# Expert weights of 128 tokens: scattered through DRAM by indirect DMAs in place of one-hot matmuls

## The chip, the cores and the metric

One core of a Trainium2 chip. The metric is device microseconds of one execution; three executions of the kernel before were timed.

## The reference

A decoder layer over 256 tokens of width 1024: modulated RMSNorm, two token mixers (pooling and attention) merged by gates, output projection, and then the part that the change touches, a product-key expert layer with 128 x 128 = 16,384 experts:

```python
q = (hf @ w_q).reshape(T, 8, 2, 128)
s = jnp.einsum('thpd,hpnd->thpn', q, sub_keys)
sv, si = lax.top_k(s, 16)
cand = sv[:, :, 0, :, None] + sv[:, :, 1, None, :]
cand_idx = si[:, :, 0, :, None] * 128 + si[:, :, 1, None, :]
cv, ci = lax.top_k(cand.reshape(T, 8, 256), 16)
expert = jnp.take_along_axis(cand_idx.reshape(T, 8, 256), ci, axis=-1)
g = jax.nn.softmax(cv, axis=-1)
a = gelu(einsum('cd,chkd->chk', x_c, u_tab[expert]))
out = einsum('chk,chkd->cd', g * a, v_tab[expert])
```

Each token picks 8 x 16 = 128 experts, each with a softmax weight.

## The kernel before, in words

The kernel gathers nothing. It computes the activation of all 16,384 experts for all tokens, multiplies by a weight that is zero where an expert was not picked, and multiplies by the whole table v. The stages, one after another on TensorE (PE): the input projections; 16 gate tiles (L517 to L527), with attention, pooling and the modulation dots run beside them in slices; 8 branch tiles; 8 output tiles; 16 query tiles with scores; 128 **u tiles** (the loop at L877); 128 **v tiles** (the loop at L941); the end.

Every weight tile is 128 x 1024 fp32. SP's queue loads it into `raw`, ACT rounds it into `whi` (L95), DVE takes the rest into `wlo` (L96), and PE multiplies with both. `Feed` (L107) keeps two tiles ahead; `raw`, `whi` and `wlo` have three buffers each in the u and v stages.

A u tile i makes 24 matmuls of 256 columns (`product`, L341) into one PSUM bank and a Gelu into `act[:, i, :]`, of shape 128 experts x 256 tokens. The weights must come into that layout, expert j on the partition, i and token along it. For that the selection (`selection`, `best`) runs on DVE in slices between the other steps: `Side` holds a generator whose yields are costs, and every tile adds a credit (SIDE_Q, SIDE_U) that buys slices. Before, it treats 4 heads for both halves of the tokens (tt = 1 and 0) as soon as their scores are there, then the other 4 heads. When it is done, `turn_picks` (L742) transposes both halves of the picks by 3 matmuls each, and then, one group of 4 tokens (GRP) per u tile, for 64 u tiles:

- `rows_of`: DVE compares a row of numbers with the picks and writes one-hot matrices `oh` (L760);
- `weigh_rows`: ACT scales one of them by the softmax weights, 4 instructions (L774);
- `spread`: PE multiplies the one-hots, 4 products of 128 x 128 by 128 in fp32, 8 matmuls in the trace (L780); the result is the 128 x 128 weight matrix of each token, in PSUM;
- `meet` (L790): DVE multiplies the act rows that are done; `wait_for_act` (L794): ACT puts the weights into the rows that are not done yet, and `late_mult` (L874) multiplies those by their Gelu when it comes.

A v tile i makes 16 matmuls (L938, L939) into eight accumulators. `weigh_act` splits two rows of act into a `w` tile (tag "w", three buffers, shared with `oh`) two v tiles ahead.

The order of instructions is the program's own on SP and POOL, on DVE from the branch stage on, and on PE and ACT in the u and v stages. POOL's queue carries 24 fetches of modulation weights (`mod_sections`, L362; `mraw`, three buffers), and between them copies `tick` of one column (`after`, L385) that wait for a gate, branch or score tile so that the queue keeps step with PE. The fetched `mraw` are consumed on DVE (L171).

Of the kernel before, what the change touches and what calls it, by code (L numbers as in the profile page):

```python
# [9 lines left out]
F32 = mybir.dt.float32  # L10
# [9 lines left out]
P = 128  # L20
# [13 lines left out]
LAG = 3  # L34
GRP = 4


# [14 lines left out]
MOD_G = 1.5  # L52
MOD_O = 1
SIDE_Q = 1.6
SIDE_U = 1.45
# [3 lines left out]
def layer_kernel(ctx: ExitStack, tc: tile.TileContext, A):  # L59
# [327 lines left out]
    after(h1[:, KD - 1, 1, 0:1].bitcast(F32))  # L387

    mask = const_load("mask", "mask", [P, P], mix)
    ident16 = mix.tile([P, P], BF16, name="ident16")  # L390
# [126 lines left out]
    for m in range(16):  # L517
        hi, lo = split(load(A["w_gate"][m]))
        ps = bank(f"gate{m}")
        product(ps[:, :T], hi, lo, h1, range(KD), step=lambda: side.add(SIDE_A / 2))  # L520
        S.activation(gate[:, m, :], ps[:, :T], AF.Tanh, scale=0.5)
        side.add(SIDE_A / 2)
        if m > 1:
            after(gate[:, m - 2, 0:1])
        if m == FIRST - 2:
            mods_side.add(0.5)
        if m >= FIRST:  # L527
            mods_side.add(MOD_G)
# [12 lines left out]
    for m in range(KD):  # L541
# [15 lines left out]
        if m > 0:  # L557
            after(merged[:, m - 1, 1, 0:1].bitcast(F32))

    warm = post.tile([P, 1], F32, name="warm")  # L560
# [117 lines left out]

    def selection(h):
        for tt in (1, 0):  # L680
            yield from pairs(tt, slice(h, h + GH))
        for h0 in range(h, h + GH, HG):
            for tt in (1, 0):
                yield from best(tt, h0)

    def best(tt, h0):
# [40 lines left out]
        V.tensor_copy(e[:, 0], ef[:, hs].rearrange("p h k -> p (h k)"))  # L727
        V.tensor_scalar(e[:, 1], e[:, 0], 7, None, op0=ALU.logical_shift_right)
        V.tensor_scalar(e[:, 2], e[:, 0], NK - 1, None, op0=ALU.bitwise_and)
        V.tensor_copy(g_e[tt][:, :, sl], e[:, 1:3])  # L730
        yield 0.6


    g_e = [scratch(2, P) for tt in range(2)]
    g_w = [scratch(P) for tt in range(2)]
    picks = big.tile([P, 3, T], F32, name="picks")
    row = big.tile([P, NK], F32, name="row")
# [3 lines left out]
    def turn_picks():  # L741
        for tt in range(2):  # L742
            ps = bank(f"picks{tt}")
            for c, src in enumerate((g_e[tt][:, 0, :], g_e[tt][:, 1, :], g_w[tt])):
                PE.transpose(ps[:, c * P : (c + 1) * P], src, ident)
            S.activation(
                picks[:, :, tt * P : (tt + 1) * P], ps[:, : 3 * P].rearrange("p (c t) -> p c t", c=3), AF.Copy
            )

    spreads = {}
    groups = T // GRP

# [60 lines left out]
    def chosen(j):  # L815
        side.extend(halves(j))
        if j % (2 * GH) == 2 * GH - 1:
            side.extend(selection((j + 1) // 2 - GH))

# [3 lines left out]
    def queries(m):  # L823
        qTs.append(work.tile([P, T], F32, tag="t", name=f"qT{m}", bufs=2))
        S.activation(qTs[m], ps_q[m][:, :T], AF.Copy)
        if m > 0:
            score(m - 1, qTs[m - 1])
            after(scores[:, m - 1, 0, 0:1])
        if m > SLAG:
            j = m - SLAG - 1  # L830
            chosen(j)
        side.add(SIDE_Q)

# [23 lines left out]

    ws = {}


# [18 lines left out]
    for i in range(NK):  # L879
# [27 lines left out]
        if some or LAG <= ready <= LAG + 1:  # L907
            rows_of(met + 1 if some else ready - LAG)
        if i == NK - 1:
            weigh_act(0)  # L910
# [30 lines left out]
    for i in range(NK):  # L941
# [4 lines left out]
        else:  # L946
            last.append((i, hi, lo, ws[i]))
        feed.ahead()
        if i % 2 == 0 and i + 2 < NK:
            weigh_act(i + 2)  # L950
        if i == 3:
            S.activation(warm2, eps, AF.Sqrt)
# [127 lines left out]
```

## Time and profile before

| | us |
|---|---|
| median of 3 executions | 1055.78 (1052.14 to 1056.24) |
| the profiled execution, its own time | 1057.16 |
| its span, first to last instruction | 1055.1 |
| PE busy | 1028.0 |
| DVE busy | 766.3 |
| ACT busy | 586.3 |
| POOL busy | 39.9 |

The span is what the profile shows; the execution's own time has 2.06 us around it. Busy PE means that matmuls are in flight; since PE is busy nearly all the time, a stage is read by what each of its tiles costs on PE and by whether another engine comes near its pace.

### The profile page before, as it was taken

To read this page: it belongs to the slowest core of one execution; us is meant where nothing else is said; L and a number is where in the kernel's file an instruction comes from. 1 tells how busy PE (TensorE), PEld (TensorE's weight loads), DVE (VectorE), ACT (ScalarE), POOL (GpSimd) and SP (SyncE) were. 2 spreads that over 40 slices of the span, in tenths; PEclk is the share of its full clock that TensorE was granted. 3 is DMA by queue.
4 is the path that set the end of the run, shared out by engine and by line. 5 is a ranking of instruction groups with operands and counts; after the bars stand their busy time and mean duration, and the time that the engine had idled before them with its cause. 6 is when DMAs were issued, how large, how long until landed. Compare 5 with 4: busy or idle time off the path is not lost.

```text
span 1055.1 us, 18956 instructions
## 1 busy us (share of the span) xinstructions
PE 1028.0 (97%) x7352; PEld 958.6 (91%) x7352; DVE 766.3 (73%) x1440; ACT 586.3 (56%) x1104; POOL 39.9 (4%) x69
## 2 busy tenths in 40 slices
PE   6999989899999999999999999999999999999997
PEld 4878989899999999999999999988888888888886
DVE  7966768797999998777788888555556555555555
ACT  4465444545664566777777777454444444444444
POOL 0012312011000000000000000000000000000000
PEclk8999989999999999999999999999999999999999
DMA  9977856365566656444444444566666665566651
GB/s 331 340 244 250 296 180 215 130 195 155 175 188 184 185 175 187 154 140 141 142 141 142 143 142 144 187 219 219 203 203 211 206 203 192 183 184 191 184 183 57
DMA packets 55965, 199.01 MB, mean 189 GB/s; under 512 B 7106, under 2 KB 7234, under 8 KB 55876
## 3 DMA queue, kind: packets, MB, share of 16 engines
q1 hardware_dynamic: 52420, 185.23, 55.0%
q0 software_dynamic: 3456, 12.58, 3.3%
q8 instruction: 57, 0.93, 0.4%
q14 instruction: 32, 0.26, 0.1%
HBM read 196.73 MB, written 1.05 MB: 187 GB/s over the span
## 4 chain that ended last, share of the span: by engine, by line
PE 90%; DVE 5%; ACT 2%; issue 1%; DMA 1%; SPq 0%; DVEq 0%; ACTq 0%; POOLq 0%; POOL 0%
PE acc L938 23%; PE acc L939 11%; PE u L347 10%; PE u L345 10%; PE u L346 10%; PE spread L780 5%; DVE wlo L96 2%; PE in L302 1%; PE in L303 1%; PE in L304 1%; PE gate L345 1%; PE gate L346 1%; PE gate L347 1%; PE q L345 1%; PE q L347 1%
## 5 line engine op out<-in xcount | busy, mean ns | idle before, releaser
L96 DVE TENSOR_TENSOR wlo<-raw,whi 128x1024 fp32r<-128x1024 f32 x320 | 390.8, 1223 | 238.1 <-ACT whi L95 237.9
L95 ACT ACTIVATE whi<-raw 128x1024 fp32r<-128x1024 f32 x320 | 338.2, 1059 | 256.7 <-PE acc L938 187.2
L938 PE MATMUL acc<-w,whi 128*128 128x512 f32 x1024 | 362.7, 399 | 0.8 <-DVE w L96 0.8
L345 PE MATMUL u<-h,whi 128*128 128x256 f32 x1024 | 293.4, 286 | 0.0
L347 PE MATMUL u<-h,wlo 128*128 128x256 f32 x1024 | 288.0, 281 | 1.0 <-DVE wlo L96 1.0
L939 PE MATMUL acc<-w,wlo 128*128 128x256 f32 x1024 | 287.8, 281 | 0.0
L346 PE MATMUL u<-h,whi 128*128 128x256 f32 x1024 | 287.8, 281 | 0.0
L938 PEld LDWEIGHTS acc<-w,whi 128*128 128x128 f32 x1024 | 192.4, 188 | 48.8 <-DVE w L96 1.0
L347 PEld LDWEIGHTS u<-h,wlo 128*128 128x128 f32 x1024 | 193.0, 189 | 1.4 <-DVE wlo L96 1.4
L939 PEld LDWEIGHTS acc<-w,wlo 128*128 128x128 f32 x1024 | 193.4, 189 | 0.0
L345 PEld LDWEIGHTS u<-h,whi 128*128 128x128 f32 x1024 | 193.1, 189 | 0.0
L346 PEld LDWEIGHTS u<-h,whi 128*128 128x128 f32 x1024 | 193.1, 189 | 0.0
L774 ACT ACTIVATE oh<-oh,picks 128x128 f32<-128x128 f32 x256 | 82.0, 407 | 0.0
L760 DVE TENSOR_TENSOR oh<-row,picks 128x1024 f32<-128x1024 f32 x64 | 78.0, 1219 | 0.0
L917 ACT ACTIVATE act<-u 128x256 f32<-128x256 f32 (+32 forms) x121 | 39.4, 325 | 58.2 <-PE u L347 58.0
L780 PE MATMUL spread<-oh 128*128 128x128 f32 x512 | 67.4, 275 | 0.0
L780 PEld LDWEIGHTS spread<-oh 128*128 128x128 f32 x512 | 62.6, 191 | 0.0
L914 ACT ACTIVATE gl<-u 128x256 f32<-128x256 f32 (+32 forms) x70 | 20.1, 288 | 73.6 <-PE u L347 66.9
L171 DVE SCALAR_TENSOR_TENSOR mraw<-mraw,c_act 128x1024 f32<-128x1024 f32 x32 | 39.0, 1219 | 12.8 <-DMA mraw<-in_w_mod 12.8
L96 DVE TENSOR_TENSOR w<-act,w 128x512 fp32r<-128x512 f32 x64 | 43.8, 685 | 0.0
L345 PE MATMUL gate<-h,whi 128*128 128x256 f32 x128 | 39.4, 308 | 0.2 <-ACT whi L95 0.2
L95 ACT ACTIVATE w<-act 128x512 fp32r<-128x512 f32 x64 | 39.4, 616 | 0.0
(254 smaller groups left out, 1191.9 us busy)
## 6 DMA issues: line engine op xcount, KB each, us to landing
raw<-in_u SPq DMA_DIRECT2D x128, 512.0 KB, 3.5
raw<-in_v SPq DMA_DIRECT2D x128, 512.0 KB, 3.6
mraw<-in_w_mod POOLq DMA_DIRECT2D x24, 512.0 KB, 4.9
raw<-in_w_gate SPq DMA_DIRECT2D x16, 512.0 KB, 4.7
raw<-in_w_q SPq DMA_DIRECT2D x16, 512.0 KB, 4.0
raw<-in_w_mod SPq DMA_DIRECT2D x8, 512.0 KB, 5.5
mraw<-in_w_mod SPq DMA_DIRECT2D x8, 512.0 KB, 6.6
raw<-in_w_qk SPq DMA_DIRECT2D x8, 512.0 KB, 6.7
```

The costliest lines, as they stand in the source:

```text
L95: S.activation(hi, t, AF.Copy)
L96: V.tensor_tensor(lo, t, hi.bitcast(F32), op=ALU.subtract)
L171: V.scalar_tensor_tensor(w, w, 1.0, c_act, op0=ALU.mult, op1=ALU.mult, accum_out=out)
L345: PE.matmul(o, hi[:, sl], hT[:, k, 0, 0:n], start=(j == 0), stop=False)
L346: PE.matmul(o, hi[:, sl], hT[:, k, 1, 0:n], start=False, stop=False)
L347: PE.matmul(o, lo[:, sl], hT[:, k, 0, 0:n], start=False, stop=(j == last))
L760: V.tensor_tensor(oh, row[:, None, None, :].to_broadcast([P, 2, GRP, NK]), picks[:, :2, sl, None].to_broadcast([P, 2, GRP, NK]), op=ALU.is ...
L774: S.activation(oh[:, 0, j, :], oh[:, 0, j, :], AF.Copy, scale=picks[:, 2, t : t + 1])
L780: PE.matmul(ps[:, j * NK : (j + 1) * NK], oh[:, 1, j, :], oh[:, 0, j, :], start=True, stop=True)
L917: S.activation(act[:, i, n:], ps[:, n:T], AF.Gelu)
L938: PE.matmul(acc[m], hi[:, sl], w, start=(i == 0), stop=False)
L939: PE.matmul(acc[m][:, T:], lo[:, sl], w[:, 0, :], start=False, stop=(i == NK - 1))
```

## The change

The second half of the tokens (tt = 1, tokens 128 to 255) gets its weights another way. A DRAM tensor `wt` of 128 x 128 x 128 floats (8 MB) is zeroed early by 16 DMAs on POOL's queue, each a 512 KB write from a 128 x 128 tile of zeros read eight times over (`clear`), bought by credits at the gate, branch and query tiles. The selection is reordered: all 8 heads of tt = 1 first, then those of tt = 0. As soon as a pair of heads of tt = 1 is selected, `place` issues 16 indirect DMAs per head on POOL, each of 128 single floats, one per partition, to addresses in `g_at`, adding to what is there (two heads may pick the same expert). That is 128 indirect DMAs. Only tt = 0 is spread by matmuls: 32 groups in place of 64. In the v stage, SP's queue fetches `wt` back in 16 pieces of 8 rows (`fetch`, 512 KB, into a "w" buffer), and DVE multiplies 8 half rows of act by each (`weigh_half`).

```diff
+IW = 8
+CLR_G = 0.25
+CLR_B = 0.3
+CLR_Q = 1
...
+    def clear():
+        for q in range(16):
+            G.dma_start(A["wt"][:, 8 * q : 8 * q + 8, :], zero[:, None, :].to_broadcast([P, 8, P]))
+            yield 1
+    clear_side = Side(clear())
...
-    def selection(h):
-        for tt in (1, 0):
-            yield from pairs(tt, slice(h, h + GH))
+    def selection(tt, h):
+        yield from pairs(tt, slice(h, h + GH))
         for h0 in range(h, h + GH, HG):
-            for tt in (1, 0):
-                yield from best(tt, h0)
+            yield from best(tt, h0)
+            if tt == 1:
+                for h1 in range(h0, h0 + HG):
+                    place(h1)
...
+        else:
+            V.tensor_scalar(e[:, 1], e[:, 0], NK - 1, 14, op0=ALU.bitwise_and, op1=ALU.logical_shift_left)
+            V.tensor_scalar(e[:, 2], e[:, 0], 7, 7, op0=ALU.logical_shift_right, op1=ALU.logical_shift_left)
+            V.tensor_tensor(e[:, 1], e[:, 1], e[:, 2], op=ALU.bitwise_or)
+            V.tensor_tensor(g_at[:, sl], e[:, 1], token.to_broadcast([P, n]), op=ALU.bitwise_or)
...
+    def place(h):
+        rows = A["wt"].rearrange("j i (t o) -> (j i t) o", o=1)
+        mine = []
+        for s in range(h * TOPK, (h + 1) * TOPK):
+            d = G.indirect_dma_start(
+                out=rows, out_offset=bass.IndirectOffsetOnAxis(ap=g_at[:, s : s + 1], axis=0),
+                in_=g_w[1][:, s : s + 1], in_offset=None, compute_op=ALU.add,
+            )
+            for e in mine:
+                tc.declare_no_dep(d.ins, e.ins, reason="experts of one head differ, and so do tokens")
+            mine.append(d)
...
-    groups = T // GRP
+    groups = P // GRP
...
         if j % (2 * GH) == 2 * GH - 1:
-            side.extend(selection((j + 1) // 2 - GH))
+            side.extend(selection(1, (j + 1) // 2 - GH))
+        if j == 2 * H - 1:
+            side.extend(*(selection(0, h) for h in range(0, H, GH)))
...
+    def fetch(i):
+        wts[i] = work.tile([P, IW, P], F32, tag="w", name=uid("wt"), bufs=3)
+        nc.sync.dma_start(wts[i], A["wt"][:, i : i + IW, :])
+    def weigh_half(i):
+        a = act[:, i : i + IW, P:]
+        V.tensor_tensor(a, a, wts.pop(i), op=ALU.mult)
...
+        if i == NK - 4:
+            fetch(0)
+        if i == NK - 2:
+            weigh_half(0)
...
         feed.ahead()
+        if i % IW == IW // 2 and i + IW // 2 < NK:
+            weigh_half(i + IW // 2)
         if i % 2 == 0 and i + 2 < NK:
             weigh_act(i + 2)
+        if i % IW == 0 and i + IW < NK:
+            fetch(i + IW)
```

What moves, in three places. First POOL's queue late in the gate stage, where the fetches `mraw` stand between copies; before:

```order
L385 COPY tick<-gate 128x1
L362 DMA mraw_1339<-in_w_mod 128x1024
L385 COPY tick<-gate 128x1
L362 DMA mraw_1392<-in_w_mod 128x1024
L362 DMA mraw_1395<-in_w_mod 128x1024
```

and now:

```order
L389 COPY tick<-gate 128x1
L396 DMA wt<-zero 128x8x128
L366 DMA mraw_1343<-in_w_mod 128x1024
L389 COPY tick<-gate 128x1
L366 DMA mraw_1396<-in_w_mod 128x1024
```

One of the 16 zeroing DMAs now stands ahead of a fetch. Four are issued in the gate stage, a fifth at its end, two in the branch stage, nine with the queries. The second place is DVE in the middle of the u stage (`wlo` is the split of a u tile, `act` here is scratch of the selection), at the end of the fourth and last pair of heads of tt = 1:

```order
L739 TENSOR_REDUCE act<-g_w_2201 128x2
L740 RECIPROCAL act<-act 128x2
L741 TENSOR_TENSOR g_w_2201<-g_w_2201,act 128x32
L743 CAST act<-act 128x32
L749 TENSOR_SCALAR act<-act 128x32
L750 TENSOR_SCALAR act<-act 128x32
L751 TENSOR_TENSOR act<-act 128x32
L752 TENSOR_TENSOR g_at<-act,token 128x32
L686 CAST act<-act 128x128
L687 TENSOR_SCALAR act<-act 128x4x16
L100 TENSOR_TENSOR wlo_4276<-raw_4273,whi_4275 128x1024
```

The four writes of `g_at` release 32 indirect DMAs each; between them and the first `oh` there are 54, 49, 31 and 26 splits of tiles. The selection of tt = 0 begins only behind the fourth. The third place is SP's queue in the v stage; before it has a load per tile, now every eighth tile a fetch between two of them:

```order
L89 DMA raw_9100<-in_v 128x1024
L89 DMA raw_9123<-in_v 128x1024
L906 DMA wt_9132<-wt 128x1024
L89 DMA raw_9150<-in_v 128x1024
L89 DMA raw_9172<-in_v 128x1024
```

The fetch for rows i + 8 stands behind the load of v tile i + 2 and ahead of that of i + 3, and takes the buffer of the `w` tile of rows i - 2 and i - 1. On PE the order is the old one less three transposes of picks and the last 32 groups of spread matmuls; the first spread stands at the same u tile.

## Rows read from the trace of the kernel before

**Rows 1.** The page: span, and each engine's busy time.

```profile
span 1055.1 us, 18956 instructions
...
PE 1028.0 (97%) x7352; PEld 958.6 (91%) x7352; DVE 766.3 (73%) x1440; ACT 586.3 (56%) x1104; POOL 39.9 (4%) x69
```

**Rows 2.** Chain that ended last: shares by line.

```profile
PE acc L938 23%; PE acc L939 11%; PE u L347 10%; PE u L345 10%; PE u L346 10%; PE spread L780 5%; DVE wlo L96 2%; PE in L302 1%; PE in L303 1%; PE in L304 1%; PE gate L345 1%; PE gate L346 1%; PE gate L347 1%; PE q L345 1%; PE q L347 1%
```

**Rows 3.** Table by stage: busy us (instructions), granted clock, DMA share, GB/s.

```profile
core 0: us, PE busy (x) PEld busy (x) DVE busy (x) ACT busy (x) POOL busy (x), PEclk, DMA share, GB/s
...
258.70:350.00 91.30, 91.30 (x774) 91.30 (x773) 87.14 (x278) 51.41 (x75) 0.00 (x0) 1.00 0.59 181
350.00:416.00 66.00, 64.96 (x547) 64.55 (x546) 61.40 (x168) 41.71 (x58) 0.00 (x0) 1.00 0.59 180
422.00:658.80 236.80, 236.80 (x2030) 236.80 (x2030) 189.21 (x252) 173.51 (x507) 0.00 (x0) 1.00 0.46 143
680.00:864.00 184.00, 184.00 (x1042) 159.46 (x1043) 108.97 (x117) 87.17 (x101) 0.00 (x0) 1.00 0.67 212
864.00:1040.00 176.00, 176.00 (x1002) 152.72 (x1000) 95.76 (x98) 81.61 (x95) 0.00 (x0) 1.00 0.57 177
```

**Rows 4.** Chain in order of time, picks, first and last spread: start us, us, what.

```profile
416.47 0.66 PE picks L745 x6
422.82 0.89 PE spread L780 x8
...
658.23 0.89 PE spread L780 x8
```

**Rows 5.** Timeline of PE, first matmuls of two tiles without spread: start us, us.

```profile
664.64 0.28 PE L345 MATMUL u<-h,whi 128*128 128x256 f32 x1
...
667.48 0.28 PE L345 MATMUL u<-h,whi 128*128 128x256 f32 x1
```

**Rows 6.** The line that fetches on POOL's queue: ns min/median/max, landing us.

```profile
L362 POOL DMA_DIRECT2D mraw<-in_w_mod x24: 527/527/681, 76.5 to 183.7; - x24
...
DMA to landing us min/median/max: 3.8/4.9/7.5
```

**Rows 7.** Chain in the gate stage, in order of time: start us, us, what.

```profile
125.62 6.73 DMA mraw<-in_w_mod
...
133.61 0.40 DVE mixed L497
...
136.65 1.22 PE mix L495 x2
137.87 0.21 PE gate L345
```

**Rows 8.** POOL's small copies between gate tiles: ns min/median/max.

```profile
L385 POOL COPY tick<-gate x14: 183/456/1266, 73.3 to 137.9; 128x1 f32<-128x1 f32 x14
```

**Rows 9.** DVE's groups from 260 to 412 us: busy us, mean ns | idle.

```profile
L96 DVE TENSOR_TENSOR wlo<-raw,whi 128x1024 fp32r<-128x1024 f32 x52 | 63.3, 1217 | 8.0 <-ACT whi L95 8.0
...
L728 DVE TENSOR_SCALAR act<-act 128x32 int32<-128x32 int32 x7 | 1.3, 182 | 0.2
```

**Rows 10.** Loads of one line on SP's queue, 864 to 1030 us.

```profile
L85 SPq DMA_DIRECT2D raw<-in_v x58: 327/328/328, 866.1 to 1027.2; - x58
...
DMA to landing us min/median/max: 3.3/3.6/4.5
```

**Rows 11.** Timelines of ACT, then of DVE, in the v stage.

```profile
900.49 1.06 ACT L95 ACTIVATE whi<-raw 128x1024 fp32r<-128x1024 f32 x1 [1.76 <-PE acc L938]
...
903.32 1.06 ACT L95 ACTIVATE whi<-raw 128x1024 fp32r<-128x1024 f32 x1 [1.25 <-PE acc L938]
...
901.58 1.23 DVE L96 TENSOR_TENSOR wlo<-raw,whi 128x1024 fp32r<-128x1024 f32 x1 [1.60 <-ACT whi L95]
```

**Rows 12.** The page's main DMA queue, and its slowest class of large loads.

```profile
q1 hardware_dynamic: 52420, 185.23, 55.0%
...
raw<-in_w_qk SPq DMA_DIRECT2D x8, 512.0 KB, 6.7
```

More of the change, by code (lines that the diff above doesn't have):

```diff
@@ L524, in layer_kernel @@
             after(gate[:, m - 2, 0:1])
+        clear_side.add(CLR_G)
         if m == FIRST - 2:
@@ L558, in layer_kernel @@
             after(merged[:, m - 1, 1, 0:1].bitcast(F32))
+        clear_side.add(CLR_B)
     warm = post.tile([P, 1], F32, name="warm")
@@ L727, in best @@
         V.tensor_copy(e[:, 0], ef[:, hs].rearrange("p h k -> p (h k)"))
-        V.tensor_scalar(e[:, 1], e[:, 0], 7, None, op0=ALU.logical_shift_right)
-        V.tensor_scalar(e[:, 2], e[:, 0], NK - 1, None, op0=ALU.bitwise_and)
-        V.tensor_copy(g_e[tt][:, :, sl], e[:, 1:3])
+        if tt == 0:
+            V.tensor_scalar(e[:, 1], e[:, 0], 7, None, op0=ALU.logical_shift_right)
+            V.tensor_scalar(e[:, 2], e[:, 0], NK - 1, None, op0=ALU.bitwise_and)
+            V.tensor_copy(g_e[:, :, sl], e[:, 1:3])
+        else:
[3 more added lines that the diff above has]
+            V.tensor_tensor(g_at[:, sl], e[:, 1], token.to_broadcast([P, n]), op=ALU.bitwise_or)
         yield 0.6
-    g_e = [scratch(2, P) for tt in range(2)]
-    g_w = [scratch(P) for tt in range(2)]
-    picks = big.tile([P, 3, T], F32, name="picks")
+    g_e = scratch(2, P)
+    g_w = [scratch(P), keep.tile([P, P], F32, name="g_w1")]
+    picks = big.tile([P, 3, P], F32, name="picks")
     row = big.tile([P, NK], F32, name="row")
@@ L741, in turn_picks @@
     def turn_picks():
[L742 to L747, printed above, removed]
-            )
+        ps = bank("picks")
+        for c, src in enumerate((g_e[:, 0, :], g_e[:, 1, :], g_w[0])):
+            PE.transpose(ps[:, c * P : (c + 1) * P], src, ident)
+        S.activation(picks, ps[:, : 3 * P].rearrange("p (c t) -> p c t", c=3), AF.Copy)
+    g_at = keep.tile([P, P], I32, name="g_at")
+    token = keep.tile([P, 1], I32, name="token")
+    G.iota(token, pattern=[[0, 1]], base=0, channel_multiplier=1)
+    def place(h):
[5 more added lines that the diff above has]
+                in_=g_w[1][:, s : s + 1], in_offset=None, compute_op=ALU.add,
+            )
+            for e in mine:
+                tc.declare_no_dep(d.ins, e.ins, reason="experts of one head differ, and so do tokens")
+            mine.append(d)
     spreads = {}
-    groups = T // GRP
+    groups = P // GRP
     def rows_of(g):
@@ L827, in queries @@
             score(m - 1, qTs[m - 1])
-            after(scores[:, m - 1, 0, 0:1])
+            if not clear_side.done:
+                after(scores[:, m - 1, 0, 0:1])
+        clear_side.add(CLR_Q)
         if m > SLAG:
@@ L858, in layer_kernel @@
     ws = {}
+    wts = {}
+    def fetch(i):
[4 more added lines that the diff above has]
+        V.tensor_tensor(a, a, wts.pop(i), op=ALU.mult)
     def weigh_act(i):
@@ L1073 @@
         aps[name] = nc.dram_tensor(f"in_{name}", a.shape, mybir.dt.from_np(a.dtype), kind="ExternalInput").ap()
+    aps["wt"] = nc.dram_tensor("wt", (NK, NK, P), F32, kind="Internal").ap()
     aps["c_act"] = nc.dram_tensor("c_act", (1, D), F32, kind="Internal").ap()
```

## The prediction

> **What bounds the kernel now.** The page comes first: TensorE (PE) is busy 1028.0 of 1055.1 us, DVE 766.3, ACT 586.3, POOL 39.9 [rows 1]. The chain of work that ended last says the same by line: v matmuls 34%, u matmuls 30%, and, the term of this change, the spread matmuls 5% [rows 2]. Then the table by stage, since a share of the whole hides a stage in which another engine is tight [rows 3]. From 422 to 659 us, where the spreads run, PE is never idle, DVE is busy 189.2 of 236.8 us and ACT 173.5: nobody else binds, so a matmul taken out there is time. From 259 to 416 us, the stage of the selection, PE is also full, but DVE is busy 87.1 of 91.3 us and then 61.4 of 66.0: 8.8 us of air in 157. From 680 us on DVE has 41 to 46% free and the DMA engines are at a share of 0.67, later 0.57.
>
> **What the change removes.** In the chain, first and last spread start at 422.82 and 658.23 us [rows 4]; there are 64, so a u tile with its spread takes 235.41 / 63 = 3.737 us. The first matmuls of two tiles without one stand 2.84 us apart [rows 5]. One spread thus costs 0.897 us; the chain's own piece says 0.89. Thirty-two of them go: 28.6 us. Three of the six transposes of the picks go too, half of 0.66 us [rows 4]: 0.3 us. Together **28.9 us**, all on PE, in a stage where PE alone sets the pace. The comparisons, scalings and multiplications that DVE and ACT lose with them are worth nothing by themselves, since PE covered them. In the v stage PE does the same as before.
>
> **What it adds, part by part.**
>
> *Zeroing.* Sixteen writes of 512 KB on POOL's queue. The nearest row is the fetch of 512 KB in 128 pieces, which held POOL for 0.53 us and landed after 3.8 to 7.5 us [rows 6]; a zeroing write is cut into 1024 pieces, so POOL needs between 0.53 and, were it by the piece, 4.2 us. It matters where POOL's queue is waited for: late in the gate stage the chain goes through a fetch issued at 125.62 that ends in a `mixed` step of DVE and a PE that starts again at 136.65, with its next matmuls at 0.21 us a piece [rows 7]. Two zeroing writes stand a little ahead of that. Each can delay it by its time on POOL and by its own transfer. A packet of the main queue costs 0.55 x 16 x 1055.1 / 52420 = 177 ns on average [rows 12], so 512 KB, 128 packets over 16 engines, take 1.4 us. Bounds: 0 (POOL is busy 4% of the time, so its queue may have the spare) and 2 x (3.7 + 1.4) = 10 us. I take **2.8 us**, the two transfers, since 0.53 us is the measured issue. The nine at the query tiles hold only POOL's copies, for which no engine waits.
>
> *Selection in another order.* The same slices with the same credits, so the spread begins at the same u tile. Each pair of heads of tt = 1 has one more small DVE step, 0.18 us [rows 9]: 4 x 0.18 = **0.7 us**, counted in full because DVE has no air there.
>
> *128 indirect DMAs.* On POOL, which has nothing else to do from 259 us on; nobody waits for them but the first fetch of `wt`. By the splits counted in the order, the four groups of 32 are released about 54, 49, 31 and 26 tiles before the picks at 416 us [rows 4], at 2.84 us a tile near 263, 277, 328 and 342 us. SP's queue reaches its first fetch at u tile 124, near 638 us with 28.9 saved. The last 64 have 310 us, 4.8 us each; POOL's time for a fetch of 128 pieces is 0.53 us [rows 6], and eight may be in flight. So **0 us** on the path. What they take from DVE is the open question. A copy of one column on POOL takes anything from 0.18 to 1.27 us [rows 8] while DVE's splits keep a mean of 1.217 us [rows 9]: it is POOL that waits for DVE. Lower end 0; upper end, DVE held for every issue: 128 x 0.53 = 68 us, less the air of 8.8, so 59 us. I take 0, by the row of the splits. The Trainium skill ("SBUF — State Buffer", SBUF: two separate sides) speaks against this: VectorE and GpSimd share a pair of SBUF ports under an exclusive lock, held for the whole instruction by whichever starts first, when a VectorE instruction with two SBUF inputs meets a GpSimd one that reads SBUF. The copies agree with the half of it in which GpSimd waits; that VectorE waits is shown by no row here.
>
> *The v stage.* Sixteen multiplications on DVE of 1024 elements with two inputs, like a split: 1.22 us each, 19.5 us in all, beside 155 us of idle DVE [rows 3]. Sixteen more fetches in SP's queue raise its traffic by an eighth. The point is their wait: fetch i + 8 takes the buffer of the `w` tile that PE uses up to tile i - 1, and the load of tile i + 3 is queued behind it. That load used to go out over two tiles earlier. Tiles are 2.83 us apart, and a split ends 2.3 us after PE frees its buffers (900.49 to 902.81) [rows 11]. From the moment PE ends tile i - 1, the load has three tiles, 8.5 us, less one issue of 0.33 and the split of 2.3: it may take 5.8 us to land. It lands after 3.6 us, at most 4.5 [rows 10]; so **0 us**, with an upper end below.
>
> **Sum**, against the profiled execution's own 1057.16 us: - 28.9 + 2.8 + 0.7 = 1031.8. The median of the three runs is 1.4 us lower, so the forecast is **1030 us**, 25.7 us (2.4%) off 1055.78.
>
> **The rivals.**
>
> *Slower: POOL holds DVE.* If each indirect DMA, which must read its 128 addresses from SBUF, keeps DVE from its two-input steps for its 0.53 us of issue, the selection stage, whose splits feed PE, grows by 59 us: 1030 + 59 = 1089. It decides from (25.7 + 8.8) / 128 = 0.27 us of DVE per indirect DMA on; below 0.07 the air hides it. For it: DVE's 8.8 us of air [rows 3] and 52 splits in 157 us [rows 9]. Against: the splits were not longer beside POOL's copies. It is the rule of the Trainium skill cited above. Chance 0.13.
>
> *Tiny pieces crowd the loads.* 16,384 floats by DMA are 1024 per DMA engine. At the 177 ns of an average packet [rows 12] they need 181 us of every engine, on top of a share of 0.59 [rows 3], 90 us, of the 153 us from 263 to 416. It decides from (153 - 90) / 1024 = 62 ns a piece; at 100 ns loads of u would be 39 us late in sum: 1069. Against: nearly all packets of that row carry 4 KB, and here 4 bytes. Chance 0.08.
>
> *The fetches stall the v tiles.* If fetch and load together land like the slowest loads of the page, 6.7 us [rows 12], each of 15 fetches makes PE wait 0.9 us: 13 us, 1043. Against: those loads belong to the start of the program, these run at a DMA share of 0.67 at most [rows 3]. Chance 0.09.
>
> *The weights come too late.* If indirect DMAs ran one after another, 0.53 + 4.9 us each [rows 6], 128 would end near 960 us and the first fetch, with all loads behind it, 320 us late: 1350. Against: only a head's first DMA waits for all before it. Chance 0.03.
>
> That the removed matmuls are not on the path can be ruled out by the stage's row [rows 3].
>
> **How the numbers follow.** Forecast 0.67; rivals 0.13, 0.08, 0.09, 0.03. Half a per cent, 5.3 us, is about what a measurement of this kernel can tell from no change. Faster by more: forecast and stalled v tiles, 0.76. Within it: the milder forms of the first two rivals, 0.06. Slower: their rest and the late weights, 0.18. Range: low, no cost at all and the scatter of the runs below their median, 1055.8 - 28.9 - 3.6 = 1023; high, zeroing at 10 and v stalls at 13, with a mild hold of DVE, 1057. That leaves out about 0.2.
>
> **What would show it.** Right: 32 spreads, PE full from the first spread to the end of u and about 29 us less of it; the selection stage as long as before, splits still at 1.22 us; v tiles 2.83 us apart. Wrong: PE waiting for `wlo` between 263 and 416 us, or DVE idle beside POOL's indirect DMAs (first rival); landings of u loads far over 3.5 us there (second); gaps every eighth v tile (third); SP standing at the first fetch (fourth); or a longer hole near 125 to 137 us, if the zeroing costs more than I took.

## The result, and the profile after

The changed kernel takes 1016.55 us in the median (four runs, 1011.15 to 1023.04), the kernel before beside it 1053.96: ratio 0.9649, 95% interval 0.9584 to 0.9713. That is 37 us less where 25.7 were forecast, and below the low end of the range, 1023. The profiled execution took 1015.11 us, against 1057.16 of the one before. (One execution of E5, 1970.89 us, and the only one of E7, 2580.37 us, were disturbed as a whole and are left out below.)

The page of the changed kernel: span, busy times, the queue of POOL's DMAs, shares of the chain by line.

```profile
span 1013.3 us, 18432 instructions
...
PE 986.1 (97%) x7093; PEld 917.8 (91%) x7093; DVE 728.4 (72%) x1396; ACT 548.5 (54%) x950; POOL 270.6 (27%) x208
...
q0 software_dynamic: 24192, 21.05, 10.4%
...
PE acc L994 23%; PE acc L995 12%; PE u L351 8%; PE u L349 8%; PE u L350 8%; DVE wlo L100 4%; PE spread L817 3%; DMA mraw<-in_w_mod 2%; PE in L306 2%; PE in L307 1%; PE in L308 1%; PE q L351 1%; PE q L349 1%; PE q L350 1%; ACT whi L99 1%
```

Beside [rows 1, 2]: PE is still the bound at 97%, the spreads' share went from 5% to 3%, POOL went from 39.9 to 270.6 us. The same kernel by stage (columns as in [rows 3]):

```profile
core 0: us, PE busy (x) PEld busy (x) DVE busy (x) ACT busy (x) POOL busy (x), PEclk, DMA share, GB/s
255.20:347.00 91.80, 90.86 (x779) 89.57 (x778) 85.95 (x287) 53.16 (x75) 65.70 (x36) 1.00 0.75 179
347.00:412.00 65.00, 63.83 (x542) 62.25 (x542) 62.56 (x175) 42.35 (x58) 50.61 (x28) 1.00 0.80 181
419.00:533.60 114.60, 114.60 (x1000) 114.60 (x999) 88.71 (x124) 87.03 (x249) 90.39 (x56) 1.00 0.70 145
536.00:638.00 102.00, 102.00 (x903) 102.00 (x902) 53.68 (x77) 52.42 (x115) 6.68 (x4) 1.00 0.68 197
641.00:803.00 162.00, 161.97 (x917) 140.43 (x918) 102.67 (x109) 76.64 (x88) 0.00 (x0) 1.00 0.67 233
810.00:990.00 180.00, 180.00 (x1041) 158.76 (x1040) 108.47 (x109) 86.07 (x98) 0.00 (x0) 1.00 0.66 215
```

In the selection stage PE has 2.1 us of gaps (0.94 + 1.17; 1.04 before) and the DMA share is 0.75 to 0.80, not 0.59, at the same 180 GB/s: the single floats take time of the DMA engines, not bandwidth. (The page's row of POOL's queue, 24,192 packets and 10.4% of the engines' span, holds the zeroing and the fetches of modulation weights too; without the indirect DMAs, in E4 below, it has 5,760 packets and 5.8%, and the share in this stage is 0.59 and 0.60.) The last two rows hold the surprise. PE is full and the granted clock 1.00 (the 2.4 GHz level) in both, yet 917 matmuls in 162 us are 5.66 a microsecond, 1041 in 180 are 5.78.

Where the 41.8 us of span went shows in PE's first matmul of each stage; the timelines of before, then of after (start us, us):

```profile
255.17 0.36 PE L345 MATMUL u<-h,whi 128*128 128x256 f32 x1
...
679.83 0.50 PE L938 MATMUL acc<-w,whi 128*128 128x512 f32 x1 [0.83 <-DVE w L96]
```

```profile
252.50 0.36 PE L349 MATMUL u<-h,whi 128*128 128x256 f32 x1
...
641.03 0.47 PE L994 MATMUL acc<-w,whi 128*128 128x512 f32 x1 [0.97 <-DVE w L100]
```

and in the chain of after, in order of time, to be set beside [rows 4, 7]:

```profile
121.11 0.91 POOL wt L396
122.02 8.10 DMA mraw<-in_w_mod
...
135.96 0.70 PE mix L507 x2
...
419.05 0.89 PE spread L817 x8
...
533.07 0.89 PE spread L817 x8
```

| stretch | before | after | difference | forecast |
|---|---|---|---|---|
| start to first u matmul | 255.17 | 252.50 | -2.7 | +2.8 |
| to first spread | 167.65 | 166.55 | -1.1 | +0.4 |
| to first v matmul | 257.01 | 221.98 | -35.0 | -28.6 |
| to the end of the span | 375.3 | 372.3 | -3.0 | 0 |

Every line is better than forecast. The third splits in two: 28.6 us are the 32 spreads, and 6.4 us come from u tiles that the change doesn't touch. A tile with its spread takes (533.07 - 419.05) / 31 = 3.678 us where it took 3.737 [rows 4], and the 39 tiles behind the last spread take (641.03 - 533.07 - 0.89 - 0.97) / 39 = 2.72 us where [rows 5] have 2.84: 31 x 0.059 + 39 x 0.12 = 6.5 us.

In nanoseconds: before, successive u matmuls start 115 to 123 ns apart (mean 118.4), and so do the 256-column matmuls of the gate, branch, output and query tiles. After, they start 113.3 or 117.9 ns apart, one of the two for whole tiles, and change over at a disturbance (a spread, a wait). A pair of v matmuls (512 and 256 columns) takes 353.3 ns throughout before; after, 353.3 until 808 us and 346.7 from there. At that point PE stood for 70 ns, and this is the timeline of PE in after:

```profile
807.52 0.40 PE L994 MATMUL acc<-w,whi 128*128 128x512 f32 x1
807.76 0.28 PE L995 MATMUL acc<-w,wlo 128*128 128x256 f32 x1
807.87 0.40 PE L994 MATMUL acc<-w,whi 128*128 128x512 f32 x1
808.11 0.35 PE L995 MATMUL acc<-w,wlo 128*128 128x256 f32 x1
808.30 0.40 PE L994 MATMUL acc<-w,whi 128*128 128x512 f32 x1
808.53 0.28 PE L995 MATMUL acc<-w,wlo 128*128 128x256 f32 x1
```

The starts of L994 are 0.35 us apart, then once 0.43, since a load of v had landed late behind a fetch. Some 540 pairs at 6.67 ns less are 3.6 us: from its first to its last matmul the v stage takes 361.1 us, before 364.7. The fourth line of the table has 3.0, since what follows the last v matmul took 0.6 us longer.

What the change adds, in after (ns min/median/max, first and last start), and DVE's splits beside it in the selection stage:

```profile
L779 POOL DMA_INDIRECT wt<-g_w,g_at x128: 1549/1552/2645, 264.0 to 541.5; - x128
L396 POOL DMA_DIRECT2D wt<-zero x16: 887/901/1120, 55.2 to 232.0; - x16
L906 SPq DMA_DIRECT2D wt<-wt x16: 326/326/327, 624.4 to 955.1; - x16
```

```profile
L100 DVE TENSOR_TENSOR wlo<-raw,whi 128x1024 fp32r<-128x1024 f32 x53 | 65.0, 1227 | 4.4 <-ACT whi L99 4.1 <-issue 0.3
```

An indirect DMA holds POOL for 1.55 us, three times the 0.53 that I took, and 128 of them end near 543 us, 81 us ahead of the first fetch. The splits take 1227 ns beside them, 1217 before [rows 9].

### The profile page after: what moved, and what is told of

Same layout as the page of the kernel before. It is cut to its first block, busy times and chain, and to the rows that moved or that the text cites. A ratio compares the mean times of both kernels' runs of the same rounds, so it can differ in the third digit from the quotient of the medians.

```text
span 1013.3 us, 18432 instructions
## 1 busy us (share of the span) xinstructions
PE 986.1 (97%) x7093; PEld 917.8 (91%) x7093; DVE 728.4 (72%) x1396; ACT 548.5 (54%) x950; POOL 270.6 (27%) x208
## 3 DMA queue, kind: packets, MB, share of 16 engines
q0 software_dynamic: 24192, 21.05, 10.4%
## 4 chain that ended last, share of the span: by engine, by line
PE 82%; DVE 11%; DMA 2%; ACT 2%; issue 2%; POOL 0%; SPq 0%; DVEq 0%; POOLq 0%; ACTq 0%
PE acc L994 23%; PE acc L995 12%; PE u L351 8%; PE u L349 8%; PE u L350 8%; DVE wlo L100 4%; PE spread L817 3%; DMA mraw<-in_w_mod 2%; PE in L306 2%; PE in L307 1%; PE in L308 1%; PE q L351 1%; PE q L349 1%; PE q L350 1%; ACT whi L99 1%
## 5 line engine op out<-in xcount | busy, mean ns | idle before, releaser
L994 PE MATMUL acc<-w,whi 128*128 128x512 f32 x1024 | 359.1, 395 | 1.0 <-DVE w L100 1.0
L349 PE MATMUL u<-h,whi 128*128 128x256 f32 x1024 | 286.9, 280 | 0.2 <-ACT whi L99 0.2
L350 PE MATMUL u<-h,whi 128*128 128x256 f32 x1024 | 283.8, 277 | 0.0
L779 POOL DMA_INDIRECT wt<-g_w,g_at x128 | 220.7, 1724 | 87.4 <-issue 36.3
L994 PEld LDWEIGHTS acc<-w,whi 128*128 128x128 f32 x1024 | 191.9, 187 | 45.6 <-PE u L351 1.1
L970 ACT ACTIVATE gl<-u 128x128 f32<-128x128 f32 (+16 forms) x70 | 17.9, 255 | 79.0 <-issue 54.3
L973 ACT ACTIVATE act<-u 128x256 f32<-128x256 f32 (+11 forms) x128 | 43.0, 336 | 30.6 <-PE u L351 29.0
L811 ACT ACTIVATE oh<-oh,picks 128x128 f32<-128x128 f32 x128 | 41.0, 406 | 0.0
L797 DVE TENSOR_TENSOR oh<-row,picks 128x1024 f32<-128x1024 f32 x32 | 39.0, 1220 | 0.0
L351 PE MATMUL gate<-h,wlo 128*128 128x256 f32 x128 | 36.3, 284 | 1.3 <-DVE wlo L100 1.3
```

Of the source, the lines that this page charges most:

```text
L349: PE.matmul(o, hi[:, sl], hT[:, k, 0, 0:n], start=(j == 0), stop=False)
L350: PE.matmul(o, hi[:, sl], hT[:, k, 1, 0:n], start=False, stop=False)
L351: PE.matmul(o, lo[:, sl], hT[:, k, 0, 0:n], start=False, stop=(j == last))
L779: d = G.indirect_dma_start(out=rows, out_offset=bass.IndirectOffsetOnAxis(ap=g_at[:, s : s + 1], axis=0), in_=g_w[1][:, s : s + 1], in_off ...
L797: V.tensor_tensor(oh, row[:, None, None, :].to_broadcast([P, 2, GRP, NK]), picks[:, :2, sl, None].to_broadcast([P, 2, GRP, NK]), op=ALU.is ...
L811: S.activation(oh[:, 0, j, :], oh[:, 0, j, :], AF.Copy, scale=picks[:, 2, t : t + 1])
```

## The experiments

The questions: does the removal give 28.6 us; what changed the pace of untouched matmuls; what did the additions cost. "Distance" below is the place in SBUF of the moving operand (h in u, w in v) less that of whi, modulo 512 bytes, as the built program lays them out; wlo lies a multiple of 512 from whi. Before: 224 in u, 0 in v. After: 192 and 0, because the new tiles `g_w1`, `g_at` and `token` push whi and wlo up by 1056 bytes, which is 32 modulo 512, while h stays. w comes to lie 480 bytes lower, since `picks` is half as big now; that is 32 modulo 512 too, so in v the distance is kept.

### E1, E2: 32 bytes more ahead of whi

In the kernel before (E1) and in the changed one (E2):

```diff
     tick = keep.tile([P, 1], F32, name="tick")
+    pad = keep.tile([P, 8], F32, name="pad")
+    V.memset(pad, 0.0)
```

> The kernel before with one more tile of 32 bytes in the pool that lies ahead of whi and wlo; nothing else. In the two profiles the granted clock is 1.00 in the u stage of both, yet successive matmuls of one u tile start 116 to 123 ns apart before (mean 118.5) and 113 or 118 apart after the change. The change's three new tiles push whi and wlo up by 1056 bytes, which is 32 modulo 64, while h stays. Theory A (place in SBUF): the cadence follows from where whi, wlo and h lie relative to each other modulo 64 bytes, so this shift alone gives 113 or 118 ns and saves 6 to 15 us, 1039 to 1048 in the median, with the spreads themselves unchanged. Rival B (traffic): the cadence follows from the work that the change takes off DVE, ACT and PSUM; then the starts stay 116 to 123 ns apart and the time is 1054 within 3. Rival C (chance of the execution): the cadence differs from one execution to the next of the same kernel; then runs scatter over 1040 to 1056.

> The changed kernel with the same 32 bytes more, so whi and wlo lie a multiple of 64 bytes from where they were before. Theory A: u matmuls go back to 116 to 123 ns, a u tile without spread from 2.72 to 2.84 us, one with a spread from 3.68 to 3.74, and the time rises by 8 to 14 us to 1024 to 1031, near the 1030 forecast. Rival B: 113 or 118 ns stay, 1016 within 4. Rival C: 1011 to 1030, scattered.

E1 took 1048.61 us (10 runs) beside 1055.89, ratio 0.994 (0.9907 to 0.9973), just above the 1048 that I expected at most; its u matmuls start 113.3 or 117.9 ns apart, and its u stage takes 419.3 us, 5.3 less than before. E2 took 1020.29, ratio 0.9698 (0.9629 to 0.9768); its u matmuls are back at 118.3 on average, none under 115. Matmuls in 15 us of u tiles without spreads (columns as in [rows 3]), in before, in E1 and in after:

```profile
661.00:676.00 15.00, 15.00 (x130) 15.00 (x128) 8.34 (x12) 6.74 (x11) 0.00 (x0) 1.00 0.55 173
```

```profile
650.50:665.50 15.00, 15.00 (x134) 15.00 (x134) 8.93 (x13) 6.74 (x11) 0.00 (x0) 1.00 0.56 173
```

```profile
560.00:575.00 15.00, 15.00 (x135) 15.00 (x134) 8.53 (x12) 7.12 (x16) 0.00 (x0) 1.00 0.69 200
```

So theory A holds in its main point and rival B falls: 32 bytes alone, with no other edit, give the kernel before 0.6% and take the faster pace from the changed one. (E2's time by itself shows no loss: its interval overlaps that of the changed kernel.) E2's gain (from PE's first spread matmul to its first v matmul, 229.2 us against 257.2) is 28.0 us, near the forecast's term. Its time is below my 1024 to 1031, since its v stage ran at the faster pace for most of the way (650 to 800 us: 867 matmuls, 851 at the pace of before).

### E3: half of the spreads, and nothing in their place

```diff
-    groups = T // GRP
+    groups = P // GRP
```

> The kernel before with only the first 32 of its 64 groups spread: the weights of the second 128 tokens are left out, and nothing is put in their place, no DRAM, no indirect DMA, no fetch. It measures the first term of the sum by itself. Forecast's own step: 32 x 0.897 = 28.6 us, 1025 in the median, u matmuls still 116 to 123 ns apart. Rival B (traffic): the matmuls get faster with the DVE and ACT work gone, 113 or 118 ns in the tiles after the last spread, and the time is 1014 to 1020.

1023.45 us beside 1055.89, ratio 0.9737 (0.9668 to 0.9806; the kernel before scattered from 1044 to 1060 there). First spread to first v, as for E2: 228.5 us, 28.7 less than before. u matmuls 118.4 ns on average with half of the DVE and ACT work of the spreads gone, v pairs 353.3 throughout. The term is right to a tenth of a microsecond in the profile, and rival B is out a second time. E3 lacks all of the additions and still is slower than the changed kernel. PE (us, busy (matmuls), clock, DMA share, GB/s) in the tiles behind the last spread and in two stretches of v, for E3, then for after:

```profile
560.00:610.00 50.00, 50.00 (x425) 1.00 0.65 188
650.00:800.00 150.00, 150.00 (x851) 1.00 0.70 213
815.00:965.00 150.00, 150.00 (x851) 1.00 0.63 186
```

```profile
560.00:610.00 50.00, 50.00 (x444) 1.00 0.68 197
650.00:800.00 150.00, 150.00 (x851) 1.00 0.66 228
815.00:965.00 150.00, 150.00 (x867) 1.00 0.65 213
```

### E4: no indirect DMAs

```diff
-            if tt == 1:
-                for h1 in range(h0, h0 + HG):
-                    place(h1)
```

> The changed kernel without its 128 indirect DMAs; the zeroing, the new order of the selection and the fetches stay. The weights of the second 128 tokens are left out (they stay zero). Forecast's own step: the indirect DMAs cost nothing on the path, so 1016.5 within 4. Rival (POOL holds DVE, or tiny pieces delay loads of u): the chain of after spends 11% on DVE and PE has gaps in the selection stage; they go, the stage from 264 to 419 us gets 2 to 8 us shorter, 1008 to 1014.

1010.7 us, ratio 0.9599 (0.9534 to 0.9663): the interval overlaps that of the changed kernel, so the times alone settle nothing. In the profiles, first u matmul to first spread takes 164.9 us without them, and 166.4 to 167.7 in the six profiles of kernels with them that keep whi at distance 192 and leave the u stage as it is (after, E5, E6, E8, E17, E18). By this one profile the indirect DMAs cost some 2 us there (1.5 to 2.8), not 0, and neither 59 nor 39.

### E5, E6, E8: the yardstick, no fetch, zeroing elsewhere

E5 is the changed kernel again. E6 leaves out `fetch` and `weigh_half` in the v stage and at its start; E8 issues all zeroing at the query tiles:

```diff
-        if i % IW == IW // 2 and i + IW // 2 < NK:
-            weigh_half(i + IW // 2)
...
-        if i % IW == 0 and i + IW < NK:
-            fetch(i + IW)
```

```diff
-CLR_G = 0.25
-CLR_B = 0.3
+CLR_G = 0
+CLR_B = 0
```

> The changed kernel once more, unaltered, as the yardstick on the chip of the three runs beside it and as a test of rival C (chance of the execution). Theory A (place in SBUF): its u matmuls start 113 or 118 ns apart again in this execution, never 116 to 123; the time is 1011 to 1023. Rival C: this profile shows another cadence in u than the first one.

> The changed kernel without the fetches of wt and the multiplications by them in the v stage; the zeroing and the indirect DMAs stay. The weights of the second 128 tokens are left out. In after, PE stood for some 70 ns at 808.1 us, behind a load of v that landed late behind a fetch, and from there on the pairs of v matmuls took 346.7 ns in place of 353.6. Theory A': the fetches' small delays are what changes the cadence of v; without them all pairs take 353.6 ns, the v stage 364.7 us and not 361.2, and the kernel is no faster than the changed one, up to 4 us slower. Rival (forecast's rival of stalled tiles): the fetches cost time; without them the v stage is shorter than 361 us. Rival (chance): the cadence changes in mid-stage here too.

> The changed kernel with all 16 zeroing DMAs issued at the query tiles, none in the gate and branch stages. It measures the forecast's second term. Forecast's own step: the two that stand ahead of a late fetch cost 2.8 us there, so the gate stage's hole shrinks and the time is some 3 us below the yardstick of the same chip. Rival: the fetches of modulation weights land late by themselves (in the half-spread run, without any zeroing, u began 3 us sooner, in the kernel before 3 us later, with the same code up to there), so no difference beyond 2 us.

E5: 1012.37 us in the median of three, ratio 0.9574 (0.9538 to 0.961). Its u matmuls are 113.3 or 117.9 ns apart again, so the kind of pace belongs to the kernel, not to the execution; but after the last spread it stayed at 117.9, where the first profile had 113.3, and its v stage was fast from the start. Which of the two paces falls is chance (as much of rival C is true); which two there are is not. E6: 1019.49, ratio 0.965 (0.9615 to 0.9685): without the fetches every v pair takes 353.3 ns, as theory A' said, and the kernel is no faster; that it is slower is clear beside E5 alone, not beside the other runs of the changed kernel. PE in E5, then in E6, in u and in two stretches of v, and in E8 in the two stretches of v:

```profile
560.00:610.00 50.00, 50.00 (x427) 1.00 0.63 185
650.00:800.00 150.00, 150.00 (x868) 1.00 0.67 233
815.00:965.00 150.00, 150.00 (x853) 1.00 0.63 209
```

```profile
560.00:610.00 50.00, 50.00 (x427) 1.00 0.62 188
650.00:800.00 150.00, 150.00 (x851) 1.00 0.67 211
815.00:965.00 150.00, 150.00 (x850) 1.00 0.63 186
```

```profile
650.00:800.00 150.00, 150.00 (x851) 1.00 0.65 225
815.00:965.00 150.00, 150.00 (x851) 1.00 0.63 208
```

E8 has all the fetches and 353.3 ns throughout v, so they don't always bring the faster pace, and E6 beside E5 settles little. Where the pace changes says more. In after, E2, E4, E5 and E18 it changes in mid-stage, eight times in all, each time in v tile 59, 75 or 107, whose load stands in SP's queue right behind a fetch. In the five profiles that have neither fetches nor disturbed tiles (before, E1, E3, E6, E10) it never changes. The pace with which v starts is another matter: it was 353.3 in those five, and with fetches, at the same distance, 346.7 in E2, E4, E5, E17 and E18 and 353.3 in after, E8 and E11. What decides that is open.

E8: 1016.87, ratio 0.9648 (0.96 to 0.9696): no gain. PE leaves the gate stage's hole at 134.81 us, in E5 at 135.72, in E3, without any zeroing, at 133.24, in a second profile of before (E10) at 136.81. By that pair zeroing in the gate stage costs about 1 us, as much as the one zeroing that stands in the chain of after, but the hole's end moves by 3.6 us between executions of the same code.

```profile
134.81 0.70 PE mix L507 x2
```

```profile
135.72 0.70 PE mix L507 x2
```

### E7, E9: disturbing single v matmuls; E10: before again

The kernel before with eight disturbances, each in one or two pairs of one v tile; E7 and E9 are the same kernel, E10 is before unaltered:

```diff
+KICKS = {(8, 0): "R", (24, 0): "S", (40, 0): "L", (56, 0): "U", (72, 0): "R", (72, 1): "R", (88, 0): "R", (104, 0): "S", (116, 0): "L"}
...
+        cuts = {"S": (0, 256, 512), "U": (0, 128, 512)}.get(kick, (0, 512))
+        lcuts = (0, 128, 256) if kick == "L" else (0, 256)
...
+        for part in ((low, high) if kick == "R" else (high, low)):
+            part()
```

> The kernel before with the order of single v matmuls disturbed at tiles 8, 24, 40, 56, 72, 88, 104 and 116: a pair turned round (8, 88; two at 72), the 512 columns cut in 256 + 256 (24, 104) or 128 + 384 (56), the 256 columns cut in 128 + 128 (40, 116). The arithmetic is the same. Theory A' (the cadence is a state which a short disturbance switches and which then stays): between the disturbances pairs take either 353.6 or 346.7 ns, for whole stretches of 16 tiles, and some of the eight switch it; the stage is 0 to 7 us shorter than 364.7. Rival (the late half of the v stage is faster in after because of its data or its traffic): nothing switches, 353.6 throughout, 1055 within 4.

> The kernel before with disturbed v tiles once more (8 and 88: a pair turned round; 72: two pairs; 24 and 104: 512 columns cut 256 + 256; 56: 128 + 384; 40 and 116: 256 columns cut 128 + 128), since its first execution was disturbed as a whole. Theory A': pairs take 353.6 or 346.7 ns for whole stretches, some of the disturbances switch, the stage is 0 to 7 us shorter than 364.7. Rival: 353.6 throughout.

> The kernel before once more, for a second profile of it. Theory A: u matmuls 116 to 123 ns apart again, u stage 423 us, v pairs 353.6 throughout. The half-spread run has the same code up to the first spread and began u at 249.3 us, the profiled execution of before at 255.2: if that is chance, this one lies anywhere from 249 to 256; if the first profile is typical, 255.

E7, left out, tells nothing. E9 took 1051.43 us (one run), its v stage 362.7 us from first to last matmul, E10's 364.7. PE between the disturbances of E9:

```profile
700.00:740.00 40.00, 40.00 (x228) 1.00 0.68 213
747.00:787.00 40.00, 40.00 (x228) 1.00 0.66 211
792.00:832.00 40.00, 40.00 (x228) 1.00 0.68 211
837.00:877.00 40.00, 40.00 (x233) 1.00 0.62 199
882.00:922.00 40.00, 40.00 (x233) 1.00 0.61 188
926.00:966.00 40.00, 40.00 (x228) 1.00 0.62 186
971.00:1001.00 30.00, 30.00 (x172) 1.00 0.59 182
1005.00:1031.00 26.00, 26.00 (x152) 1.00 0.46 146
```

Two paces and nothing between: 228 matmuls in 40 us (353.3 ns a pair) or 233 (346.7). The cut of 128 + 384 switched to fast, the turned pair at tile 88 back, the cut of 128 + 128 switched at tile 116 and not at 40. The same disturbance doesn't always do the same, so something else counts too, perhaps the phase at which it falls. E10 (1055.63 us) has 116 to 123 ns in u and 353.3 throughout v, like the first profile, and began u at 253.7 us; E9, of the same code up to v, at 251.7, E3 at 249.3: the first line of the table above, -2.7, is within what chance moves. Some of it can be the layout, since the gate tiles have 256-column matmuls too, 118.1 ns apart before and 115.5 in after.

### E11 to E16: which distance

E11 shifts whi by 64 bytes more (u 128, v 0). E12 puts whi and wlo 16 bytes into buffers of 4160 bytes. E13 and E14 shift only w (v 64 and 192), E15 and E16 both (u 64 with v 128, u 0 with v 320). E11, E15 and E16 have the edit of E1 with other sizes, E13 to E16 (E13 and E14 as their only edit) this one, with other sizes for E14 to E16:

```diff
     work = ctx.enter_context(tc.tile_pool(name="work", bufs=2, reuse_waits="tile"))
+    wpad = work.tile([P, 16], F32, name="wpad", bufs=1)
+    V.memset(wpad, 0.0)
```

and for E12 alone, with wlo likewise:

```diff
-        hi = stream.tile([P, 1024], F32R, tag="whi", name=uid("whi"), bufs=WB)
+        hi = stream.tile([P, 1040], F32R, tag="whi", name=uid("whi"), bufs=WB)[:, 4:1028]
```

> The changed kernel with 64 bytes more ahead of whi and wlo: the distance of whi, wlo and h stays 0 modulo 64 but goes from 64 to 0 modulo 128. Theory A with 64 bytes: u matmuls 113 or 118 ns apart as in the changed kernel, 1009 to 1023. Rival with 128 bytes: a third cadence, and a time outside of that on either side.

> The changed kernel with whi and wlo 16 bytes further in buffers of 4160 bytes: 16 modulo 64 from h and from w. Theory A says only that the cadence follows the distance; a value between 0 and 32 has not been seen. If any distance other than 0 costs, u matmuls take 116 to 123 ns and v pairs more than 353.6, 1024 to 1032; if only 32 does, 113 or 118 and 1009 to 1023.

> The changed kernel with the pool of the w tiles 64 bytes further on; whi, wlo and h stay. In u the distance from whi to h is 192 modulo 512 as in the changed kernel, in v that from whi to w goes from 0 to 64. So far: u matmuls take 118.4 ns at distances 224 and 160, 120.0 at 128, 113.3 or 117.9 at 192; v pairs 353.3 or 346.7 at 0. Theory D (the distance modulo 128 sets the cadence, 64 is the best): v pairs get 4 to 20 ns shorter, the v stage 4 to 20 us, 995 to 1012. Rival (the address of whi alone decides, 32 modulo 128): v is as in the changed kernel, 1009 to 1023.

> The same with 192 bytes: distance 192 in v, 64 modulo 128. Theory D with 128 bytes: the same as with 64 bytes, pair by pair. Rival with 256 or 512 bytes: another cadence than at 64. Rival (address of whi alone): 1009 to 1023.

> The changed kernel with whi and wlo 128 bytes further and w 256: distance 64 in u, 128 in v. Theory D with 128 bytes: u 113.3 or 117.9 as at 192, v 353.3 or 346.7 as at 0, 1009 to 1023. Rival with 256 or 512 bytes: other numbers in either stage.

> The changed kernel with whi and wlo 192 bytes further and w 512: distance 0 in u, 320 (64 modulo 128) in v. Theory D with 128 bytes: u 120 ns as at 128, which costs 12 to 20 us, and v as with the shift of 64, which wins 4 to 20: 1003 to 1028. Rival with 512 bytes: u at 0 is not as at 128.

| | us | ratio (95%) | u distance: ns a matmul | v distance: ns a pair |
|---|---|---|---|---|
| after | 1016.55 | 0.9649 (0.9584 to 0.9713) | 192: 113.3 or 117.9 | 0: 353.3 or 346.7 |
| E2 | 1020.29 | 0.9698 (0.9629 to 0.9768) | 160: 118.3 | 0: 353.3 or 346.7 |
| E11 | 1028.68 | 0.9738 (0.969 to 0.9787) | 128: 120.0 | 0: 353.3 |
| E13 | 1024.45 | 0.9712 (0.9682 to 0.9743) | 192: 113.3 or 117.9 | 64: 353.3 |
| E14 | 1017.33 | 0.9631 (0.9599 to 0.9664) | 192: 113.3 or 117.9 | 192: 353.3 |
| E15 | 1021.53 | 0.9674 (0.9643 to 0.9704) | 64: 117.8 | 128: 351.1 |
| E16 | 1029.92 | 0.9753 (0.9718 to 0.9789) | 0: 119.9 | 320: 353.3 |

The ns are from the starts of successive matmuls in the traces, one profile for each of the kernels from E2 on. In E14 that was the slowest of four executions, 1023.52 us where the others took 1014.81 to 1018.11, and E11's four ran from 1022.94 to 1033.3; so a second pace that the profile missed can't be excluded for either. E12 (1022.87, 0.9696, 0.9677 to 0.9716) can't be read for one distance: buffers of 4160 bytes lie 64 apart modulo 512, so its distances differ from buffer to buffer, and its v pairs run between 346 and 353 ns in a cycle of 8.4 us, three v tiles, one round of the buffers.

My theory was half wrong. Distance counts: E13, in which only w moves, has v pairs made of other intervals (231, 233 and 236 ns behind 512 columns, where distance 0 has 232, 236 and 241), though both sum up to 353.3, and E15's 351.1 are seen nowhere else. But the pattern doesn't repeat at 64 bytes (E11 falls out), nor at 128 (u at 64 has 117.8 alone, at 192 also 113.3), and the gain of 4 to 20 us in v that I worked out from u was not there: no distance tried beats the 346.7 ns seen at 0 in v. Of the distances tried in u, 192, on which the change happened to land, is the best, by these profiles. One thing stays open: h was never moved, so in u the distance can't be told from whi's own place. In v it can: in E1 and E11 whi moves together with w, and the intervals of the slower pace stay as they were before.

### E17, E18: a switch on purpose

E17 is the changed kernel with one cut of 128 + 384 columns in v tile 2 (`KICKS = {(2, 0): "U"}`, code as in E7), E18 the changed kernel beside it.

> The changed kernel with one matmul of v tile 2 (m = 0, whi) cut in 128 + 384 columns. If this cut leads to 346.7 ns from either state, the v stage begins fast in every execution and stays so until a late load: 2 to 7 us below the changed kernel's median on the same chip, and less scatter. If it only turns one state into the other, the changed kernel being in either by chance, the medians agree within 2 us.

> The changed kernel, unaltered: the yardstick of the run beside it, and its scatter. 1011 to 1023, as so far; u matmuls 113 or 118 ns apart, v pairs 353.3 or 346.7 for whole stretches.

1016.6 us (0.9635, 0.9609 to 0.9662) and 1015.31 (0.9634, 0.9595 to 0.9672): no difference. Both profiles show v fast from its start, E17 to the end, E18 until 942 us; in E17 PE stood for some 160 ns at 808.6 us, in v tile 59, and the pace stayed. The cut brought no gain, and no version of the full computation was found that beats the changed kernel by more than these intervals.

## Why the prediction was wrong

The direction was right, and the term that carried it was; the time was not in the range.

**The step that failed** is "In the v stage PE does the same as before", with its companion in the same part, where the u tiles that stay were given no term at all. I priced the 5120 matmuls of u and v, which the change doesn't touch, at nothing, as if their pace were theirs alone. In u it moved by 6.4 us, since three new tiles changed the distance between whi and h from 224 to 192 (E1 and E2 show it by 32 bytes alone); in v by 3.6 us in the profiled execution, since a short wait threw the pairs from 353.3 to 346.7 ns. That such disturbances switch the pace is shown by E9, that the fetches bring them by the tiles at which it changes; why one switches and another doesn't is open, and so is what makes two paces at all. The Trainium skill ("TensorE: Matmul & The Clock Gate", Back-to-back issue gap) gives an isolated matmul N / 2.4 + 2.5 ns; an estimate from it for 256 columns is 109 ns, and the trace has 113.3 to 120.0 by layout.

Of the 16.7 us between the sum, 1031.8, and the profiled execution, 1015.11, these two are 6.4 and, to the end of the span, 3.0. The stretch before the first u matmul has 5.5 (the zeroing, chance, perhaps some layout), the selection 1.5. Part of the 6.4 is luck: after the last spread the first profile had 113.3 ns; E5, E6, E17 and E18 had 117.9 there, and first spread to first v took 226.4 us where it took 222.1. With that pace u gives some 2 us.

**The 32 spreads.** -28.6 forecast; 28.7 less in E3, 28.0 in E2. Right, and by the working given: period of a tile with a spread less period of one without.

**Zeroing.** +2.8 forecast, about 1 by E8 beside E5, and nothing in the medians. The path was the right one: the chain of after goes through a zeroing, 0.91 us on POOL, and its fetch lands after 8.10 us where it took 6.73 before. POOL's time per DMA lay near the lower of my bounds, 0.53 and 4.2. The hole that I built on moves by 3.6 us from execution to execution; I read one execution as typical.

**The selection.** +0.7 forecast. The stretch got 1.1 us shorter, and two opposite things lie in it: faster matmuls, and some 2 us for the indirect DMAs (E4), which I had at 0. Faster matmuls give little there. The stretch took 167.8 us at 120.0 ns a matmul (E11), 167.5 at 118.3 (before) and 166.4 at 114.2 (after), by PE's own starts: the faster PE was, the more it waited (steps of over 135 ns between u matmuls held 0.2, 1.8 and 6.8 us of waiting). DVE is busy 152.9 of 162.8 us there in after, which makes it the likely limit; no run tests that.

**POOL holds DVE.** Didn't come. The splits took 1227 ns beside 128 indirect DMAs that held POOL for 1.55 us and more, 1217 before; in E5, with the same DMAs, 1219, in E4, without them, 1218. The exclusive lock that the Trainium skill states ("SBUF — State Buffer", SBUF: two separate sides) costs DVE no more than 10 ns a split here.

**Tiny pieces.** Half seen: the DMA share rose to 0.75 and 0.80, but not far enough. The 18,432 packets that after has more than E4 on POOL's queue took some 41 ns of an engine each (an estimate from the two shares, 10.4% and 5.8%), under the 62 from which the rival decides. Loads of u landed late 23 times, but 20 times in E4 as well, and 3 before.

**Fetches stall v tiles.** The loads did wait: in after, ACT stood for them 46 times in the v stage (ACT's waits, us in total, times, longest), which no row of before has:

```profile
ACT whi L99 <- DMA raw<-in_v: 89.6, 46, 4.6
```

The buffers covered it but for 70 ns of PE at 808 us, and behind those 70 ns the faster pace won 3.6 us. The rival had the mechanism and, in this execution, the wrong sign; in E4 the stand at the same tile ended the faster pace.

**Weights too late.** No: last indirect DMA at 541.5 us, first fetch at 624.4.

**The range.** Its low end allowed "no cost at all" and the scatter of the runs. Nothing in it stood for untouched work getting cheaper, though the profile showed u matmuls of one shape 115 to 123 ns apart at a granted clock of 1.00, a scatter that I never asked about.

## What to carry to other kernels

Before a change is credited or blamed, compare the starts of successive instructions of work that it doesn't touch, at equal granted clock; if they moved, the change has done more than it was made for: here it moved the layout, and disturbed a pace that has two values. A kernel that PE bounds is worth a run or two with 32 to 224 bytes of padding ahead of its weights: here 32 bytes alone gave the kernel before 0.6% and cost the changed one its faster pace. Take more than one profile of each, since one layout can show two paces. And what removing work from the engine that is the bound gives can be forecast from the periods of tiles with and without it: 28.6 us here, where 28.7 and 28.0 were measured.

## What was not expected of the hardware

At the granted clock of 1.00, 256-column fp32r matmuls start 117.8, 118.4 or 120.0 ns apart on average by where one operand lies in SBUF against the other, and at one distance (192 modulo 512) in either of two paces, 113.3 or 117.9, that last for whole tiles. Pairs of 512 and 256 columns have two such paces at distance 0, 353.3 and 346.7 ns; a wait of 70 ns, or one matmul cut in two, can switch them, and need not: a wait of 160 ns in E17 didn't. An indirect DMA of 128 floats holds POOL for 1.55 to 2.65 us.
